# Seven expert steps a layer instead of eight: the four least loaded experts share one step

## The chip, the cores and the metric

The kernel runs on one core of a Trainium2 chip. The metric is the device time of one execution in microseconds (us), the median of several runs. A core has a matrix engine (TensorE, PE in the profile, with its weight loads as PEld), a vector engine (VectorE, DVE), an activation engine (ScalarE, ACT), GpSimd (POOL) and SyncE (SP), which here issues nearly all DMA transfers from memory.

## The reference

Two blocks of a transformer on 256 tokens of width 1024. The first has two layers; each ends in a mixture of experts, and only that part is touched:

```
g_p, g_idx = top_k(softmax(t @ rg_w + rg_b), 1)          # one of 4 groups
e_sel = logits of the 4 experts of that group
top_p, top_i = top_k(softmax(e_sel), 2)                  # 2 of its 4 experts
comb[token, expert] = g_p * top_p / sum(top_p)           # 16 experts, else 0
for each expert e:                                       # width 256
    acc += ((silu(t @ wg[e]) * (t @ wu[e])) @ wd[e]) * comb[:, e]
```

Each token goes to 2 of 16 experts, so 512 token places are spread over 16 experts, unevenly. Worked out from the reference's router on its own inputs, the counts of experts 0 to 15 are 38, 34, 36, 18, 77, 39, 76, 52, 11, 13, 18, 16, 23, 23, 22, 16 in the first layer and 31, 17, 13, 25, 31, 31, 32, 44, 22, 34, 29, 31, 35, 61, 33, 43 in the second. The weights of an expert are 3 MB in fp32.

## The kernel before, in words

The function `moe` does one expert layer. It computes the router, and from it for each token and expert a rank (`rk`, which place of that expert's slots the token gets), a weight (`cw`) and for each expert a count (`cn`). An expert has `CAP` = 64 slots. A *step* handles two experts side by side: expert 0 of the pair in rows 0 to 63 of a PSUM tile, expert 1 in rows 64 to 127, by `tile_position=(0, 64 * e)`, which makes of the 128 columns of TensorE two halves that work side by side. A layer has eight steps:

- `prepare(q)`, once for two steps, makes one-hot slots (`oh`, `ow`) for four experts and gathers their tokens by matmuls (`gps`, line 535, four times 64 slots), into `xg` or `ug`.
- `up(step)` multiplies the gathered tokens by gate and up weights (`gu`, line 557): four weight chunks of 1 MB, two for the first half of the 1024 inputs (one an expert), two for the second half. Within a half the loop runs over four blocks k and, inside, over the experts. Then SiLU on ScalarE and a product on VectorE.
- `turn` transposes the result and the slot weights (`htp`); it stands in the program between the two halves of the next step's `up`.
- `down(step)` multiplies by the down weights (`yp`, line 590, two 1 MB chunks), evicts with the slot weight into a high and a low part (ScalarE line 595, VectorE line 596), and adds the rows back to their tokens by 16 matmuls into four PSUM tiles (`y`, line 599).

The program order is up(0), prepare(1), up(1), down(0), up(2), prepare(2), down(1), up(3), down(2), up(4), prepare(3), down(3) and so on: `down` of a step stands after `up` of the next one. The final order on each engine is set by the framework's planner, which runs the program against modelled costs and takes, of the instructions that it believes ready, the earliest in the program; the order that it finds is fixed in the program.

Weight chunks are read into 13 slots of 1 MB in three pools (`ring` 4, `ring_b` 7, `ring_m` 2); which pool the n-th chunk takes is fixed by the list `rings` (line 989), except those of the last step, which have pools of their own. A chunk's transfer is issued by SP in program order, once the chunk that had its slot before has been used. Steps 0 and 1 take experts 0 to 3. From step 2 on the expert's number is read by SP from `ints`, which VectorE computes: experts 4 to 15 in order, but that the (up to two) experts of most over 64 tokens are exchanged into places 14 and 15, the last step. That step's weights are kept: where any expert has more than 64 tokens, a conditional part (`overflow`, line 774) runs it again for the tokens beyond 64. `more_blocks` computes whether that is so and whether still more blocks are needed. `perm` puts ranks and weights in the same order (`rkp`, `cwp`).

Of the kernel before, what the change touches and what calls it, by code (L numbers as in the profile page):

```python
# [10 lines left out]
F32 = mybir.dt.float32  # L11
# [38 lines left out]
NC1 = _lay(C1T, [("stri", 128), ("cos2d", 128), ("sin2d", 128), ("slot", 64), ("first", 4), ("o14", 16), ("o15", 16), ("free", 16), ("ends", 2), ("less", 16)])  # L50
# [5 lines left out]
FILL = (0, 0, 0, 1, 1, 1, 0, 2, 0)  # L56

# [3 lines left out]
def build(tc, I, O):  # L61
# [3 lines left out]
    with es:  # L65
# [355 lines left out]
        def moe(layer, norm, rc, work, blocks):  # L421
# [85 lines left out]
            def slots(n, ranks, weights):  # L507

                shape = [128, n, CAP]
                oh = small.tile([128, 2, n, CAP], F32R, name="oh", tag=f"oh{n}", bufs=2 if n == 4 else 1)  # L510
                ow = small.tile([128, 2, n, CAP], F32, name="ow", tag=f"ow{n}", bufs=2 if n == 4 else 1)
                for b in range(2):
                    V.tensor_tensor(oh[:, b], C("slot").unsqueeze(1).to_broadcast(shape),
                                    ranks[:, b].unsqueeze(2).to_broadcast(shape), op=ALU.is_equal)
                    V.tensor_tensor(ow[:, b], oh[:, b].bitcast(F32),
                                    weights[:, b].unsqueeze(2).to_broadcast(shape), op=ALU.mult)
                return oh, ow
# [30 lines left out]
            def up(x_, s0, gus, between=lambda: None):  # L548

                gu = acc("gu")  # L550
                for h in range(2):
                    if h:
                        between()
                    w = [gus(h, e) for e in range(2)]
                    for k in range(4):
                        for e in range(2):
                            T.matmul(gu[64 * e:64 * e + 64, :],  # L557
                                     x_[:, 4 * h + k, s0 + 64 * e:s0 + 64 * e + 64],
                                     w[e][:, 512 * k:512 * k + 512],
                                     start=(h == 0 and k == 0), stop=(h == 1 and k == 3),  # L560
                                     tile_position=(0, 64 * e))
# [20 lines left out]
            def down(turned, dns, first, last):  # L582
                ht, back, cws = turned
                wd = [dns(e) for e in range(2)]
                yg = pair([128, D], "yg", small, bufs=2)
                for q in range(2):
                    yp = (ops if q else acc)("yp")
                    for k in range(2):
                        for e in range(2):
                            T.matmul(yp[64 * e:64 * e + 64, :],  # L590
                                     ht[:, 128 * k + 64 * e:128 * k + 64 * e + 64],
                                     wd[e][:, 1024 * k + 512 * q:1024 * k + 512 * q + 512],
                                     start=(k == 0), stop=(k == 1), tile_position=(0, 64 * e))
# [18 lines left out]
            def prepare(q):  # L612
                oh, ow = slots(4, (rkp if q else rk)[:, :, 4 * q:4 * q + 4], (cwp if q else cw)[:, :, 4 * q:4 * q + 4])
                if q == 0:
                    late = t(1, "late")
                    V.scalar_tensor_tensor(late, rk[:, :, 0:1], 0.0, rc.unsqueeze(2), op0=ALU.mult, op1=ALU.add)
                    for q_ in range(2):
                        for b in range(2):
# [10 lines left out]
            order, over, dd = (small.tile([128, 16], F32, name=n, tag=n) for n in ("order", "over", "dd"))  # L629
            top = small.tile([128, 8], F32, name="top", tag="top")  # L630
            two, sw = (small.tile([128, 2], F32, name=n, tag=n) for n in ("two", "sw"))
            V.scalar_tensor_tensor(over, cn, CAP + 0.5, C("free"), op0=ALU.is_gt, op1=ALU.mult)
            V.max(top, over)
            V.scalar_tensor_tensor(two, top[:, 0:2], 0.0, C("ends"), op0=ALU.is_equal, op1=ALU.mult)
            V.tensor_tensor(two, two, top[:, 0:2], op=ALU.add)
            V.scalar_tensor_tensor(dd, iota, two[:, 0:1], C("o15"), op0=ALU.is_equal, op1=ALU.subtract)
            V.tensor_tensor(sw[:, 0:1], iota[:, 15:16], two[:, 0:1], op=ALU.subtract)
            V.scalar_tensor_tensor(order, dd, sw[:, 0:1], iota, op0=ALU.mult, op1=ALU.add)
            V.scalar_tensor_tensor(dd, order, two[:, 1:2], C("o14"), op0=ALU.is_equal, op1=ALU.subtract)
            V.tensor_tensor(sw[:, 1:2], order[:, 14:15], two[:, 1:2], op=ALU.subtract)  # L640
            V.scalar_tensor_tensor(order, dd, sw[:, 1:2], order, op0=ALU.mult, op1=ALU.add)
            ints = small.tile([128, 16], I32, name="ints", tag="ints")
            intr = small.tile([128, 10], I32, name="intr", tag="intr")
            V.tensor_copy(ints, order)

            in2 = small.tile([128, 12, 16], F32, name="in2", tag="in2")
            perm = small.tile([128, 12, 16], F32, name="perm", tag="perm")
            shape = [128, 12, 16]
            V.tensor_tensor(perm, order[:, 4:16].unsqueeze(2).to_broadcast(shape),
                            iota.unsqueeze(1).to_broadcast(shape), op=ALU.is_equal)  # L650
# [8 lines left out]
            def more_blocks():  # L659
# [6 lines left out]
                V.tensor_scalar(ov, cn, CAP + 0.5, None, op0=ALU.is_gt)  # L666
                for n in (2, 3):
                    V.scalar_tensor_tensor(ov, cn, n * CAP + 0.5, ov, op0=ALU.is_gt, op1=ALU.add)
# [27 lines left out]
                V.tensor_tensor(prev, prev, last, op=ALU.subtract)  # L696
                picked(off, prev)
# [36 lines left out]
            def weights_of(step, h, e):  # L734

                if (step, h, e) not in loaded:
                    if step < 2:
                        c = chunk(f"gu{layer}", 4 * step + 2 * e + h) if h < 2 else chunk(f"dn{layer}", 2 * step + e)
                    else:
                        if (step, e) not in experts:  # L740
                            experts[step, e] = value(ints, 2 * step + e)
                        i = experts[step, e]
                        c = dyn(f"gu{layer}", i * 2 + h, ring_b if step == 7 else None) if h < 2 else dyn(f"dn{layer}", i, ring if step == 7 else None)
                    loaded[step, h, e] = c
                return loaded[step, h, e] if step == 7 else loaded.pop((step, h, e))

            hs = {}
            for step in range(9):
                def turned(step=step):
                    if step:  # L750
                        q, h_ = divmod(step - 1, 2)
# [1107 lines left out]
```

## Time and profile before

| | |
|---|---|
| median of 3 runs | 1513.59 us (1512.26 to 1514.64) |
| the profiled execution's own time | 1514.41 us |
| its span, first to last instruction | 1512.7 us |
| TensorE busy | 1474.8 us (97%) |
| VectorE, ScalarE, GpSimd busy | 57%, 44%, 2% |
| moved by DMA | 324.85 MB, mean 215 GB/s |
| granted TensorE clock, mean | 0.986 of full speed |

The page's share of busy time is one over the whole span. The expert layers take from about 183 to 348 us and from about 469 to 619 us of it. Times in the rows are from the span's start. An instruction's shown duration on TensorE holds its way through the pipeline, so that neighbours overlap: what it costs is the distance to the next one's start. In a row of a stretch the busy times stand in the order PE, PEld, DVE, ACT, POOL, each with its number of instructions in brackets; in a row of a timeline the start comes first, then how long the run of x instructions lasted.

### The profile page before, as it was taken

What the parts mean: (1) busy time and instruction counts of PE and PEld (TensorE: products, weight loads), DVE (VectorE), ACT (ScalarE), POOL (GpSimd) and SP (SyncE); (2) the same over time, 40 slices, a digit from 0 to 9 for tenths busy, and PEclk for the clock granted to TensorE, in tenths of its full rate; (3) what the DMA queues carried; (4) which work ended last, traced back from release to release, by engine and by line L of the source; (5) the groups of instructions that cost most, each with busy time, mean ns of one, the idle gap of its engine ahead of it and who ended that gap; (6) DMA issues with size and microseconds to landing.
All of it is one profiled execution on the core that took longest, in us unless ns stands there. A gap on an engine that the chain in (4) does not pass through costs nothing.

```text
span 1512.7 us, 25576 instructions
## 1 busy us (share of the span) xinstructions
PE 1474.8 (97%) x10412; PEld 1178.0 (78%) x10412; DVE 857.9 (57%) x1682; ACT 658.1 (44%) x1114; POOL 26.7 (2%) x59
## 2 busy tenths in 40 slices
PE   8999899989999999899999999999999999999998
PEld 3756645445986444698789999999898789999998
DVE  2765452225646222657777775555758777765554
ACT  2544311115433111556564554444565654654443
POOL 0000000000000000010000000000010000000000
PEclk9999999999999999999999999999999999999999
DMA  9974789739584986553315464554444135465540
GB/s 396 388 296 167 304 368 404 292 136 371 205 349 174 414 336 246 178 171 116 136 59 186 177 221 175 188 196 167 136 157 168 57 114 184 177 223 179 185 166 29
DMA packets 47005, 324.85 MB, mean 215 GB/s; under 512 B 5600, under 2 KB 5984, under 8 KB 8480
## 3 DMA queue, kind: packets, MB, share of 16 engines
q1 hardware_dynamic: 45360, 320.12, 55.8%
q8 instruction: 86, 1.41, 0.4%
q10 hardware_dynamic: 1296, 1.55, 0.3%
q0 software_dynamic: 224, 1.46, 0.3%
q14 instruction: 39, 0.32, 0.1%
HBM read 322.06 MB, written 1.05 MB: 214 GB/s over the span
## 4 chain that ended last, share of the span: by engine, by line
PE 56%; DVE 2%; ACT 1%; issue 0%; DVEq 0%; ACTq 0%
PE fm L162 10%; PE fm L163 10%; PE fm L161 10%; PE d L162 4%; PE d L161 4%; PE d L163 4%; PE tm L194 1%; PE tm L195 1%; PE tm L196 1%; PE sp L1486 1%; PE lf L162 1%; PE lf L163 1%; PE lf L161 1%; PE po L1475 1%; PE ptp L1469 1%; DVE sc L1359 1%
## 5 line engine op out<-in xcount | busy, mean ns | idle before, releaser
L134 DVE TENSOR_TENSOR wlo<-w,whi 128x1024 fp32r<-128x1024 f32 (+1 forms) x314 | 378.4, 1208 | 251.9 <-ACT whi L133 249.2
L133 ACT CAST whi<-w 128x1024 fp32r<-128x1024 f32 (+1 forms) x314 | 324.3, 1035 | 384.5 <-PE fm L162 230.7
L161 PE MATMUL fm<-acth,whi 128*128 128x256 f32 x592 | 169.4, 286 | 0.0
L162 PE MATMUL fm<-actl,whi 128*128 128x256 f32 x592 | 168.3, 284 | 0.0
L163 PE MATMUL fm<-acth,wlo 128*128 128x256 f32 x592 | 167.9, 284 | 0.0
L163 PE MATMUL d<-hidh,wlo 128*128 128x256 f32 x512 | 144.2, 282 | 0.0
L162 PE MATMUL d<-hidl,whi 128*128 128x256 f32 x512 | 144.0, 281 | 0.0
L161 PE MATMUL d<-hidh,whi 128*128 128x256 f32 x512 | 143.9, 281 | 0.0
L162 PE MATMUL fm<-oTl,whi 128*128 128x256 f32 x512 | 143.6, 281 | 0.0
L163 PE MATMUL fm<-oTh,wlo 128*128 128x256 f32 x512 | 143.3, 280 | 0.0
L161 PE MATMUL fm<-oTh,whi 128*128 128x256 f32 x512 | 143.1, 280 | 0.0
L162 PEld LDWEIGHTS fm<-actl,whi 128*128 128x128 f32 x592 | 112.5, 190 | 2.3 <-issue 2.3
L161 PEld LDWEIGHTS fm<-acth,whi 128*128 128x128 f32 x592 | 113.2, 191 | 1.0 <-issue 0.8
L163 PEld LDWEIGHTS fm<-acth,wlo 128*128 128x128 f32 x592 | 112.4, 190 | 1.3 <-issue 1.0
L162 PEld LDWEIGHTS fm<-oTl,whi 128*128 128x128 f32 x512 | 96.8, 189 | 0.4 <-DVE oTl L1100 0.4
L162 PEld LDWEIGHTS d<-hidl,whi 128*128 128x128 f32 x512 | 96.7, 189 | 0.4 <-DVE hidl L134 0.4
L161 PEld LDWEIGHTS fm<-oTh,whi 128*128 128x128 f32 x512 | 96.9, 190 | 0.0
L161 PEld LDWEIGHTS d<-hidh,whi 128*128 128x128 f32 x512 | 96.8, 189 | 0.1
L163 PEld LDWEIGHTS d<-hidh,wlo 128*128 128x128 f32 x512 | 96.7, 189 | 0.1
L163 PEld LDWEIGHTS fm<-oTh,wlo 128*128 128x128 f32 x512 | 96.7, 189 | 0.0
L590 PE MATMUL yp<-w,ht 128*64 128x512 f32 x272 | 84.1, 646 | 6.8 <-PEq L774 3.5
L557 PE MATMUL gu<-w,xg 128*64 128x512 f32 x288 | 70.1, 599 | 0.0
(537 smaller groups left out, 2904.5 us busy)
## 6 DMA issues: line engine op xcount, KB each, us to landing
w<-gu SPq DMA_DIRECT2D x64, 1024.0 KB, 9.3
w<-mod SPq DMA_DIRECT2D x48, 1024.0 KB, 11.2
w<-dn SPq DMA_DIRECT2D x32, 1024.0 KB, 9.7
w<-gw SPq DMA_DIRECT2D x32, 1024.0 KB, 4.8
w<-up SPq DMA_DIRECT2D x32, 1024.0 KB, 4.8
w<-dw SPq DMA_DIRECT2D x32, 1024.0 KB, 4.8
w<-tm SPq DMA_DIRECT2D x12, 1024.0 KB, 5.0
w<-oin SPq DMA_DIRECT2D x8, 1024.0 KB, 8.3
```

The lines of the kernel that those rows point to most:

```text
L133: A.copy(hi, src)
L134: V.tensor_sub(lo, src, hi.bitcast(F32))
L161: T.matmul(out, ws[0], xs[0], start=first, stop=False, skip_group_check=skip)
L162: T.matmul(out, ws[0], xs[1], start=False, stop=False, skip_group_check=skip)
L163: T.matmul(out, ws[1], xs[0], start=False, stop=last, skip_group_check=skip)
L194: T.matmul(ps, at[0], ww[0], start=first, stop=False, skip_group_check=True)
L195: T.matmul(ps, at[1], ww[0], start=False, stop=False, skip_group_check=True)
L196: T.matmul(ps, at[0], ww[1], start=False, stop=k == NK - 1, skip_group_check=True)
L557: T.matmul(gu[64 * e:64 * e + 64, :], x_[:, 4 * h + k, s0 + 64 * e:s0 + 64 * e + 64], w[e][:, 512 * k:512 * k + 512], start=(h == 0 and k ...
L590: T.matmul(yp[64 * e:64 * e + 64, :], ht[:, 128 * k + 64 * e:128 * k + 64 * e + 64], wd[e][:, 1024 * k + 512 * q:1024 * k + 512 * q + 512] ...
L1359: V.scalar_tensor_tensor(dst, rl[:, :nk], iw[:, b, h:h + 1], dst, op0=ALU.mult, op1=ALU.add)
L1469: T.transpose(tp[:, 128 * c:128 * c + 128], prs[g][:, 128 * c:128 * c + 128], ident)
```

## The change

Two sizes of step. The order of experts 4 to 15 is now a full sort on VectorE: `more_` counts for each how many of the twelve have more tokens (`key` breaks ties by number), and `RANKS` says which rank comes to which place. The four with the fewest (ranks 8 to 11) come to places 8 to 11 and form one step (step 4) with 32 slots each; the two with the most still come to the last step, which is now step 6. `up` and `down` take a number of experts n: with n = 4 each expert's tile is 32 columns wide, `tile_position=(0, 32 * e)`, and such a step reads 8 gate/up chunks and 4 down chunks. The gather is made for 64 slots an expert as before, and the step uses the first 32 of them. An expert of the four with more than 32 tokens goes to the conditional part. The prepare of the last quarter stands after up(4) as before, and its tokens are now used in step 5 and not 6.

```diff
-NC1 = _lay(C1T, [("stri", 128), ("cos2d", 128), ("sin2d", 128), ("slot", 64), ("first", 4), ("o14", 16), ("o15", 16), ("free", 16), ("ends", 2), ("less", 16)])
+NC1 = _lay(C1T, [("stri", 128), ("cos2d", 128), ("sin2d", 128), ("slot", 64), ("first", 4), ("rank", 12), ("gap", 38), ("less", 16)])
...
+STEPS = ((0, 1), (2, 3), (4, 5), (6, 7), (8, 9, 10, 11), (12, 13), (14, 15))
+PART = ((0, 0), (0, 1), (1, 0), (1, 1), (2, 0), (3, 0), (3, 1))
+LAST = 6
+RANKS = (2, 3, 4, 5, 8, 9, 10, 11, 6, 7, 1, 0)
...
-            def slots(n, ranks, weights):
+            def slots(n, ranks, weights, cap=CAP):
...
-                ow = small.tile([128, 2, n, CAP], F32, name="ow", tag=f"ow{n}", bufs=2 if n == 4 else 1)
+                ow = small.tile([128, 2 * n * CAP], F32, name="ow", tag=f"ow{n}", bufs=2 if n == 4 else 1)
+                ow = ow[:, 0:2 * n * cap].rearrange("p (b n s) -> p b n s", b=2, n=n)
...
-                    V.tensor_tensor(ow[:, b], oh[:, b].bitcast(F32),
-                                    weights[:, b].unsqueeze(2).to_broadcast(shape), op=ALU.mult)
+                    V.tensor_tensor(ow[:, b], oh[:, b, :, 0:cap].bitcast(F32),
+                                    weights[:, b].unsqueeze(2).to_broadcast([128, n, cap]), op=ALU.mult)
...
-            def up(x_, s0, gus, between=lambda: None):
...
+            def up(x_, s0, gus, between=lambda: None, n=2):
...
+                each = 128 // n
...
-                    w = [gus(h, e) for e in range(2)]
+                    w = [gus(h, e) for e in range(n)]
...
-                        for e in range(2):
-                            T.matmul(gu[64 * e:64 * e + 64, :],
-                                     x_[:, 4 * h + k, s0 + 64 * e:s0 + 64 * e + 64],
+                        for e in range(n):
+                            T.matmul(gu[each * e:each * e + each, :],
+                                     x_[:, 4 * h + k, s0 + CAP * e:s0 + CAP * e + each],
...
-                                     tile_position=(0, 64 * e))
+                                     tile_position=(0, each * e))
...
-            def down(turned, dns, first, last):
+            def down(turned, dns, first, last, n=2):
...
-                wd = [dns(e) for e in range(2)]
+                each = 128 // n
+                wd = [dns(e) for e in range(n)]
...
-                        for e in range(2):
-                            T.matmul(yp[64 * e:64 * e + 64, :],
-                                     ht[:, 128 * k + 64 * e:128 * k + 64 * e + 64],
+                        for e in range(n):
+                            T.matmul(yp[each * e:each * e + each, :],
+                                     ht[:, 128 * k + each * e:128 * k + each * e + each],
...
-                                     start=(k == 0), stop=(k == 1), tile_position=(0, 64 * e))
+                                     start=(k == 0), stop=(k == 1), tile_position=(0, each * e))
...
-                oh, ow = slots(4, (rkp if q else rk)[:, :, 4 * q:4 * q + 4], (cwp if q else cw)[:, :, 4 * q:4 * q + 4])
+                oh, ow = slots(4, (rkp if q else rk)[:, :, 4 * q:4 * q + 4], (cwp if q else cw)[:, :, 4 * q:4 * q + 4],
+                               CAP // 2 if q == 2 else CAP)
...
-            order, over, dd = (small.tile([128, 16], F32, name=n, tag=n) for n in ("order", "over", "dd"))
-            top = small.tile([128, 8], F32, name="top", tag="top")
-            two, sw = (small.tile([128, 2], F32, name=n, tag=n) for n in ("two", "sw"))
-            V.scalar_tensor_tensor(over, cn, CAP + 0.5, C("free"), op0=ALU.is_gt, op1=ALU.mult)
-            V.max(top, over)
-            V.scalar_tensor_tensor(two, top[:, 0:2], 0.0, C("ends"), op0=ALU.is_equal, op1=ALU.mult)
-            V.tensor_tensor(two, two, top[:, 0:2], op=ALU.add)
-            V.scalar_tensor_tensor(dd, iota, two[:, 0:1], C("o15"), op0=ALU.is_equal, op1=ALU.subtract)
-            V.tensor_tensor(sw[:, 0:1], iota[:, 15:16], two[:, 0:1], op=ALU.subtract)
-            V.scalar_tensor_tensor(order, dd, sw[:, 0:1], iota, op0=ALU.mult, op1=ALU.add)
-            V.scalar_tensor_tensor(dd, order, two[:, 1:2], C("o14"), op0=ALU.is_equal, op1=ALU.subtract)
-            V.tensor_tensor(sw[:, 1:2], order[:, 14:15], two[:, 1:2], op=ALU.subtract)
-            V.scalar_tensor_tensor(order, dd, sw[:, 1:2], order, op0=ALU.mult, op1=ALU.add)
+            order, key, more_ = (small.tile([128, 16], F32, name=n, tag=n) for n in ("order", "key", "more"))
+            few = small.tile([128, 24], F32, name="few", tag="few")[:, 0:16]
+            V.scalar_tensor_tensor(key, cn, 16.0, iota, op0=ALU.mult, op1=ALU.add)
+            in2 = small.tile([128, 12, 16], F32, name="in2", tag="in2")
+            perm = small.tile([128, 12, 16], F32, name="perm", tag="perm")
+            G.memset(perm, 0.0)
+            G.memset(more_, 0.0)
+            shape = [128, 12, 12]
+            V.tensor_tensor(in2[:, :, 0:12], key[:, 4:16].unsqueeze(1).to_broadcast(shape),
+                            key[:, 4:16].unsqueeze(2).to_broadcast(shape), op=ALU.is_gt)
+            V.tensor_reduce(more_[:, 4:16], in2[:, :, 0:12], axis=AX.X, op=ALU.add)
+            V.tensor_tensor(perm[:, :, 4:16], more_[:, 4:16].unsqueeze(1).to_broadcast(shape),
+                            C("rank").unsqueeze(2).to_broadcast(shape), op=ALU.is_equal)
+            shape = [128, 12, 16]
+            V.tensor_tensor(in2, perm, iota.unsqueeze(1).to_broadcast(shape), op=ALU.mult)
+            V.tensor_reduce(order[:, 4:16], in2, axis=AX.X, op=ALU.add)
...
-            V.tensor_copy(ints, order)
...
-            in2 = small.tile([128, 12, 16], F32, name="in2", tag="in2")
-            perm = small.tile([128, 12, 16], F32, name="perm", tag="perm")
-            shape = [128, 12, 16]
-            V.tensor_tensor(perm, order[:, 4:16].unsqueeze(2).to_broadcast(shape),
-                            iota.unsqueeze(1).to_broadcast(shape), op=ALU.is_equal)
+            V.tensor_copy(ints[:, 4:16], order[:, 4:16])
...
-                V.tensor_scalar(ov, cn, CAP + 0.5, None, op0=ALU.is_gt)
...
+                V.tensor_scalar(few, more_, 7.5, None, op0=ALU.is_gt)
+                V.scalar_tensor_tensor(key, few, CAP / 2, cn, op0=ALU.mult, op1=ALU.add)
+                V.tensor_scalar(ov, key, CAP + 0.5, None, op0=ALU.is_gt)
...
-                    V.scalar_tensor_tensor(ov, cn, n * CAP + 0.5, ov, op0=ALU.is_gt, op1=ALU.add)
+                    V.scalar_tensor_tensor(ov, key, n * CAP + 0.5, ov, op0=ALU.is_gt, op1=ALU.add)
...
+                V.scalar_tensor_tensor(prev, few, 0.5, prev, op0=ALU.mult, op1=ALU.add)
...
-                            experts[step, e] = value(ints, 2 * step + e)
+                            experts[step, e] = value(ints, STEPS[step][e])
...
-                        c = dyn(f"gu{layer}", i * 2 + h, ring_b if step == 7 else None) if h < 2 else dyn(f"dn{layer}", i, ring if step == 7 else None)
+                        c = (dyn(f"gu{layer}", i * 2 + h, ring_b if step == LAST else None) if h < 2 else
+                             dyn(f"dn{layer}", i, ring if step == LAST else None))
...
-                return loaded[step, h, e] if step == 7 else loaded.pop((step, h, e))
+                return loaded[step, h, e] if step == LAST else loaded.pop((step, h, e))
...
-            for step in range(9):
+            for step in range(LAST + 2):
...
-                        q, h_ = divmod(step - 1, 2)
+                        q, h_ = PART[step - 1]
+                        n = len(STEPS[step - 1])
...
-                                            lambda b: ow[:, b, 2 * h_:2 * h_ + 2].rearrange("p e s -> p (e s)"))
+                                            lambda b: ow[:, b, n * h_:n * h_ + n].rearrange("p e s -> p (e s)"))
...
-                if step < 8:
-                    q, h_ = divmod(step, 2)
-                    hs[step] = up(quarter[q][0], 128 * h_, lambda h, e: weights_of(step, h, e), turned)
+                if step <= LAST:
+                    q, h_ = PART[step]
+                    hs[step] = up(quarter[q][0], 128 * h_, lambda h, e: weights_of(step, h, e), turned,
+                                  len(STEPS[step]))
...
-                        weights_of(7, 2, e)
+                        weights_of(LAST, 2, e)
...
-                        overflow(res, cwp[:, :, 14:16], lambda h, e: weights_of(7, h, e), lambda e: weights_of(7, 2, e))
+                        overflow(res, cwp[:, :, 14:16], lambda h, e: weights_of(LAST, h, e),
+                                 lambda e: weights_of(LAST, 2, e))
...
-                    yg = down(hs.pop(step - 1), lambda e: weights_of(step - 1, 2, e), step == 1, step == 8)
-            for key in [k for k in loaded if k[0] == 7]:
+                    yg = down(hs.pop(step - 1), lambda e: weights_of(step - 1, 2, e), step == 1, step == LAST + 1,
+                              len(STEPS[step - 1]))
+            for key in [k for k in loaded if k[0] == LAST]:
...
+    put(c1, C1T, "rank", np.array(RANKS)[None])
```

## Rows read from the trace of the kernel before

**Rows 1.** Page: busy us of each engine, share of the span, instructions

```profile
PE 1474.8 (97%) x10412; PEld 1178.0 (78%) x10412; DVE 857.9 (57%) x1682; ACT 658.1 (44%) x1114; POOL 26.7 (2%) x59
```

**Rows 2.** Stretches of both expert layers: busy us (instructions), clock, DMA share, GB/s

```profile
189.90:317.70 127.80, 127.06 (x624) 58.31 (x624) 42.67 (x129) 21.04 (x38) 0.00 (x0) 1.00 0.85 339
476.60:604.50 127.90, 127.15 (x625) 58.48 (x624) 42.45 (x129) 21.03 (x38) 0.00 (x0) 1.00 0.83 329
...
200.00:270.00 70.00, 69.85 (x362) 33.92 (x362) 23.21 (x63) 12.74 (x24) 0.00 (x0) 1.00 0.99 404
```

**Rows 3.** TensorE's timeline, one late step in each layer: start us, us

```profile
287.06 7.09 PE L557 MATMUL gu<-w,ug 128*64 128x512 f32 x32
293.98 1.88 PE L590 MATMUL yp<-w,ht 128*64 128x512 f32 x4
...
296.37 3.65 PE L590 MATMUL yp<-w,ht 128*64 128x512 f32 x12
...
302.17 0.28 PE L599 MATMUL y<-back,ygh 128*128 128x256 f32 x1
302.29 0.28 PE L599 MATMUL y<-back,ygl 128*128 128x256 f32 x1
302.50 7.09 PE L557 MATMUL gu<-w,ug 128*64 128x512 f32 x32
...
573.69 7.09 PE L557 MATMUL gu<-w,ug 128*64 128x512 f32 x32
...
589.13 7.09 PE L557 MATMUL gu<-w,ug 128*64 128x512 f32 x32
```

**Rows 4.** TensorE's timeline: matmuls of 32 columns, a down in two-wide order

```profile
464.59 2.78 PE L375 MATMUL mps<-w,cpad 128*32 128x512 f32 x22
...
531.80 3.60 PE L590 MATMUL yp<-w,ht 128*64 128x512 f32 x16
```

**Rows 5.** TensorE's timeline, step 4 of the first layer, its gather, step 5

```profile
256.15 3.65 PE L557 MATMUL gu<-w,xg 128*64 128x512 f32 x16
259.74 0.74 PE L535 MATMUL gps<-oh,whi 128*128 128x256 f32 x4
...
271.75 2.79 PE L557 MATMUL gu<-w,xg 128*64 128x512 f32 x10
...
278.55 1.88 PE L590 MATMUL yp<-w,ht 128*64 128x512 f32 x4
```

**Rows 6.** SP's timeline: issues of weight chunks, and time to landing (line 717)

```profile
192.83 2.71 SPq L717 DMA_DIRECT2D w<-gu  x4
...
227.01 8.51 SPq L717 DMA_DIRECT2D w<-dn  x2
...
236.36 9.34 SPq L717 DMA_DIRECT2D w<-gu  x4
...
DMA to landing us min/median/max: 4.7/9.1/14.1
```

**Rows 7.** VectorE's timeline: the order of the experts; TensorE's next gather

```profile
187.86 0.17 DVE L633 MAX8 top<-over 128x8 f32<-128x16 f32 x1
...
191.38 0.17 DVE L644 CAST ints<-order 128x16 int32<-128x16 f32 x1
...
194.35 0.42 DVE L513 TENSOR_TENSOR oh<-cst,rkp 128x256 fp32r<-128x256 f32 x1
...
198.25 0.74 PE L535 MATMUL gps<-oh,whi 128*128 128x256 f32 x4
```

**Rows 8.** TensorE's timeline: around the conditional part, first and second layer

```profile
318.06 1.08 PE L535 MATMUL gps<-oh,whi 128*128 128x128 f32 x8
...
340.71 4.54 PE L590 MATMUL yp<-w,ht 128*64 128x512 f32 x10 [3.49 <-PEq L774]
...
604.37 0.28 PE L599 MATMUL y<-back,ygl 128*128 128x256 f32 x1
607.45 1.97 PE L590 MATMUL yp<-w,ht 128*64 128x512 f32 x4 [2.80 <-PEq L772]
```

More of the change, by code (lines that the diff above doesn't have):

```diff
@@ L1826, in host_layout @@
     put(c, CT, "inv", np.tile(np.concatenate([fr(16), fr(32), fr(8)]), 2)[None])
-    put(c1, C1T, "o14", (r(16) == 14)[None])
-    put(c1, C1T, "o15", (r(16) == 15)[None])
-    put(c1, C1T, "free", np.where(r(16) >= 4, r(16), 0)[None])
+    put(c1, C1T, "rank", np.array(RANKS)[None])
     put(c1, C1T, "less", np.tri(4, k=-1).reshape(1, 16))
-    put(c1, C1T, "ends", np.array([15, 14])[None])
     put(c1, C1T, "first", np.array([4.0, 3.0, 2.0, 1.0])[None])
```

## The prediction

> **What bounds the kernel now.** The page comes first: TensorE is busy 97% of the span [rows 1], so it looks as if TensorE's own instructions are the time. That is an average, so next come the stretches of the two expert layers, the only stage that the change touches. From 189.9 to 317.7 us TensorE works 127.06 of 127.80 us, the granted clock is 1.00 of full (its 2.4 GHz level), and the second layer repeats it to 0.1 us [rows 2]. VectorE and ScalarE work a third and a sixth of that. DMA is the second resource: over the first 70 us of it its engines are busy 99% at 404 GB/s, over the whole stretch 85% [rows 2]. TensorE is hardly ever kept waiting for a chunk all the same, as its 0.74 us of idle time leave no room for it: the 13 slots keep the weights ahead. So in this stage a TensorE instruction that goes is time that goes, as long as the weights still come in time.
>
> The timeline of TensorE then gives the price of a step. Late steps, without a gather, repeat at equal distance: from the `gu` at 287.06 to that at 302.50 in the first layer, from 573.69 to 589.13 in the second, 15.44 us both times [rows 3].
>
> **What a tile width costs.** The runs show how matmuls share the array. A run of 32 `gu` records takes 7.09 us, 16 `yp` records in two-wide order 3.60, so 16 more records take 3.49 us [rows 3, 4]; but only 4 `yp` records also take 1.88 us, which is half of 16 and not a quarter [rows 3]. These agree if two neighbours on the two halves of the array share one slot of time: (7.09 - 3.60) / 8 = 0.436 us a slot, 0.11 over, and 4 unpaired records make 4 slots, 1.85. The 12 that follow in 3.65 us fill 8 slots: 4 pairs and 4 alone. The kernel also has matmuls of 32 columns, those of the conditions, on four quarters: 22 records in 2.78 us [rows 4], that is (2.78 - 0.11) / 0.436 = 6.1 slots, four to a slot. So 64 records of a four-wide `up` fill 16 slots, as 32 records of a two-wide one do, and it costs the same 6.92 us; 32 `yp` records fill 8 slots.
>
> **The change part by part.**
>
> *One step less.* Eight steps become seven a layer. Steps 0 to 3 keep their place, step 4 is wider at equal cost, the old steps 6 and 7 follow it. What goes is one late step: 16 slots of `gu`, 12 of `yp`, one `htp`, 16 `y` matmuls and the small gaps between, 15.44 us [rows 3]. Two layers: 30.9 us. This is all on the path, as TensorE is what everything waits for [rows 2].
>
> *Order of the four-wide matmuls.* They share slots only where four experts' records stand side by side in the fixed order. In the program they do. The planner breaks that where it believes one chunk late: the late downs show it, with one expert's 4 records alone, then `htp` (which stands later in the program), then the rest, 12 slots for 8 [rows 3]. The ups of the same steps, 32 records in 7.09 us, are whole, and so is the earlier down at 531.80 [rows 4]. Step 4 asks for 8 chunks where it asked for 4, just before the place where the first split down stands (278.55, rows 5). Bounds: no split at all, and `yp` of step 4 back from 12 to 8 slots: 1.7 us less a layer than above. Or every expert by itself: `gu` in runs of 8 records of one quarter, where only the last of a run shares a slot with the first of the next, 64 - 7 = 57 slots for 16, and `yp` in runs of 4, 32 - 7 = 25 for 12: 54 slots, 23.5 us more a layer. I take the nearest row, one split of the kind at 293.98 to 296.37 in `gu` (4 slots) and the 12 slots of today in `yp`: 1.7 us a layer, 3.5 in all.
>
> The Trainium skill, in "TensorEngine Tiling (Array Packing)", section "Tiling Modes", says that changing the tile configuration, and not only the tile, drains TensorE. The step adds changes between 32 and 64 columns where neighbours were 64 wide. If each cost a whole slot, by this rule, three new ones a layer would bring the sum to about 1489. The rows have such a change too, from 128 to 64 columns: from one `y` matmul to the next it takes 0.12 us, from the last `y` to the `gu` 0.21 [rows 3], so 0.09 us a change, and by that the sum stays.
>
> *Weights in time.* The bytes are the same, 48 MB a layer, in 15.4 us less. From 192.83 us on, 38 chunks are left, the first four those of step 2 [rows 6]. At 404 GB/s [rows 2] a chunk (1.049 MB) takes 2.6 us: 99 us, so the last could land at about 292 plus its latency of 9 [rows 6], 301; the last `down` of the first layer would begin at 340.71 - 15.4 = 325 [rows 8]. In the second layer the same stream begins 286.6 us later (573.69 - 287.06), ends at about 587, and the last down begins at 607.45 - 15.4 = 592. So the stream as such does not bound, with 5 us to spare. The tightest place inside is step 4. The pool of the n-th chunk does not change, so it goes out when the n-th did before: the wide step's chunks 5 to 8 take the places of two `dn` (from 227.01) and two `gu` (from 236.36, four over 9.34 us, so by 241) [rows 6]. With the median landing that is 250, with the longest of 14.1 us 255, and the second half of `up` begins at 256.15 [rows 5]: in time. Two `dn` and the four `gu` of step 5 follow, six times 2.6 us later, by 266, and its main run begins at 271.75 [rows 5]. I take nothing for it; the price, if cover is short, is 2.6 us a chunk, at most the four chunks that step 4 asks for early: 10 us a layer.
>
> *Gather of the last quarter.* It still runs after `up` of step 4 (259.74, rows 5). Its user moves from step 6 to step 5, whose main run starts 12 us later. Nothing.
>
> *Sorting.* Between `MAX8` and the cast to `ints` VectorE ran nine small operations on 16 elements or fewer in 3.5 us, part of it evictions in between [rows 7]. New are six up to the cast: one on 16 elements, three on 144 and two on 192 elements, at 0.17 to 0.4 us each (a cast on 16 takes 0.17, an `oh` on 256 takes 0.42) [rows 7], some 1.8 us; `perm` leaves the part behind the cast. That is a change of -1 to +1 us. Behind it wait SP's first chunk of step 2 (192.83) and the one-hots of the next gather, ready at 194.35 + 0.42 while TensorE comes to that gather at 198.25: 3.5 us of cover [rows 7]. Two memsets go to an idle GpSimd (2%, rows 1). `ow` gets smaller by half for one quarter, `more_blocks` gets two operations more, both off the path. Nothing.
>
> *Sum.* The profiled execution took 1514.41 us, 1.7 over its span and 0.8 over the median of 1513.59. 1514.41 - 30.9 + 3.5 = 1487.0; against the median 1486.2. I predict 1486.
>
> **The rivals.**
>
> *The planner takes the wide step apart.* One mechanism, in the order of TensorE in step 4: its eight `gu` chunks are believed to come one by one, and the matmuls are emitted expert by expert, on one quarter at a time. For it: the split downs at and after the very place where more weights are asked for. Against it: every `up` is whole, even in steps whose down is split [rows 3], and a chunk that is believed late shows as one split, not as a run of them. It decides from 15.44 / 0.436 = 35 extra slots a layer; fully apart, it costs 23.5 us a layer and the kernel is slower: 1513.6 + 2 x (23.5 - 15.4) = 1530. Half of it, about 11 us, leaves 1505.
>
> *The stream of weights becomes the bound.* For it: DMA at 99% over 70 us [rows 2] and the same bytes in less time. Against it: the sums above. If step 4 and its successors wait for 10 us a layer, 1483 + 20 = 1503.
>
> *It does not do what it says.* 32 slots are too few, and the conditional part runs in the second layer too. There it cost 340.71 - 318.06 = 22.7 us in the first layer, of which 3 are the branch that the second layer pays as well (607.45 - 604.37) [rows 8]: 19.6 us, so 1506. Against it: the four fewest of experts 4 to 15 have 16, 16, 13, 11 tokens in the first layer and 31, 31, 29, 22 in the second; it fits by one.
>
> **How the numbers follow.** The three runs spread by 0.16%, so less than 0.2% (3 us) can't be told from no change. The forecast, seven whole or nearly whole steps at 1477 to 1495, gets 0.70. Planner apart: 0.19, of which 0.11 partly, 1495 to 1511, and 0.08 from there to 1530. Stream bound: 0.07, between the forecast and 1503. Overflow: 0.02. What I have not thought of: 0.02, slower. From 1478 to 1502 leaves out 0.05 below and about 0.14 above. Faster: 0.70 + 0.07 + 0.02 and 0.09 of the planner's partial case, 0.88; same: 0.02 of that case and 0.02 of the worse one, 0.04; slower: 0.06 + 0.02 = 0.08.
>
> **What would show it.** TensorE's timeline should have, in each layer, 64 `gu` and 32 `yp` records of 32 columns, the `gu` in 6.9 to 9 us of its time; the last down begins 14 to 17 us earlier in the first layer and twice that in the second, and all behind it moves with it. Starts in fours within a few hundredths of a us prove a slot shared by four; lone 32-column records 0.43 us apart prove the split. A wait of `gu` or `yp` for the DMA of `w` shows the stream as the bound. A second run of the conditional part shows as a gather of 128 columns at the end of the second layer. The prediction is wrong if either layer gets shorter by less than 12 us.

## The result: 20 us less where 28 were forecast

The changed kernel takes 1493.7 us (1490.45 to 1495.34, 4 runs) against 1514.12 us of the kernel before (1512.26 to 1515.65, 4 runs) on the same chip: a ratio of 0.9866, 95% interval 0.9852 to 0.9879, that is 18.3 to 22.4 us less. The forecast was 1486, with a range of 1478 to 1502. The sign and the mechanism came as forecast, but two terms of the sum were too small: broken groups of matmuls cost 8.7 us where 3.5 were reckoned, and the gathers some 2 us where nothing was. Below, a difference between two kernels is that of their ratios to the kernel before, where 0.001 is 1.5 us. The profiled execution took 1494.22 us, its span was 1492.5. A matmul of the program shows as two records in these traces: an `up` of two experts is 16 matmuls and 32 records.

The page of the changed kernel: busy us of each engine, share of the span, instructions. It answers to [rows 1]: TensorE has 21.7 us less to do and is still busy 97%.

```profile
PE 1453.1 (97%) x10370; PEld 1168.0 (78%) x10372; DVE 851.7 (57%) x1666; ACT 654.1 (44%) x1108; POOL 27.3 (2%) x63
```

A stretch of the changed kernel, columns as in [rows 2], whose row of before had the same busy time of TensorE, and a DMA share of 0.99 with 404 GB/s:

```profile
200.00:270.00 70.00, 69.85 (x378) 32.96 (x378) 22.00 (x64) 11.28 (x22) 0.00 (x0) 1.00 0.96 391
```

TensorE is as busy here as before, 69.85 of 70 us at the full clock. What it did not save must be in its own instructions, and its timeline shows where. This is step 4 of the first layer (start us, us, then the run of instructions), from its `up` to its `down`:

```profile
251.68 1.04 PE L566 MATMUL gu<-w,xg 128*32 128x512 f32 x2
...
253.57 1.05 PE L566 MATMUL gu<-w,xg 128*32 128x512 f32 x4
...
257.00 3.62 PE L566 MATMUL gu<-w,xg 128*32 128x512 f32 x26
...
261.23 1.04 PE L566 MATMUL gu<-w,xg 128*32 128x512 f32 x2
...
263.81 3.63 PE L566 MATMUL gu<-w,xg 128*32 128x512 f32 x30
267.37 1.93 PE L600 MATMUL yp<-w,ht 128*64 128x512 f32 x4
269.24 0.44 PE L580 MATMUL htp<-cst,hh 128*128 128x128 f32 x2
...
269.82 3.65 PE L600 MATMUL yp<-w,ht 128*64 128x512 f32 x12
...
275.93 7.09 PE L566 MATMUL gu<-w,ug 128*64 128x512 f32 x32
282.95 1.90 PE L600 MATMUL yp<-w,ht 128*32 128x512 f32 x4
...
285.37 3.66 PE L600 MATMUL yp<-w,ht 128*32 128x512 f32 x28
```

The `up` of step 4 has its 64 records of 32 columns, but in five pieces. With the prediction's slot (0.436 us, and 0.11 over for a run) the pieces are 2, 2, 8, 2 and 8 slots: 22, where whole groups take 16. A short run is dear: 2 records take as long as 8 could. The `down` of step 3 (267.37 and 269.82) is in two pieces with `htp` (269.24) between, 12 slots for 8, and the `up` of step 5 behind it (275.93) is whole. The `down` of step 4 is in two pieces too, 12 slots, as forecast. The second layer repeats all of this.

The same steps were not whole before either. TensorE's timeline of the kernel before: the first half of step 4's `up` (its second half is at 256.15 in [rows 5]), then step 3's `down` and the `up` of step 5:

```profile
250.07 1.07 PE L557 MATMUL gu<-w,xg 128*64 128x512 f32 x2
...
251.99 3.65 PE L557 MATMUL gu<-w,xg 128*64 128x512 f32 x14
...
262.74 1.07 PE L590 MATMUL yp<-w,ht 128*64 128x512 f32 x2
...
264.88 1.50 PE L590 MATMUL yp<-w,ht 128*64 128x512 f32 x5
...
266.64 1.89 PE L590 MATMUL yp<-w,ht 128*64 128x512 f32 x8
...
269.83 1.08 PE L557 MATMUL gu<-w,xg 128*64 128x512 f32 x4
...
275.06 3.65 PE L557 MATMUL gu<-w,xg 128*64 128x512 f32 x16
```

Step 4's `up` took 2 + 8 + 8 = 18 slots. Step 3's `down` took 2 slots at 262.74 and, with a `yp` and two early `gu` of step 5 between its runs of 5 and 8, 8 more to 268.5; the rest of step 5's `up` took 2, 6 (271.75 in [rows 5]) and 8: 26 for both, where whole groups take 24. So the change added 4 slots in the `up` of step 4 (22 for 18), and 2 in the `down` of step 3 and the `up` of step 5 (28 for 26).

At the start of a layer there is more of it. The ups of steps 0 and 1 in the changed kernel, first layer:

```profile
189.53 1.93 PE L566 MATMUL gu<-w,xg 128*64 128x512 f32 x6
...
192.53 6.22 PE L566 MATMUL gu<-w,xg 128*64 128x512 f32 x26
...
202.10 1.07 PE L566 MATMUL gu<-w,xg 128*64 128x512 f32 x2
...
204.23 3.65 PE L566 MATMUL gu<-w,xg 128*64 128x512 f32 x14
```

Six records in 1.93 us are 4 slots and 26 in 6.22 are 14, 18 for 16; 2 and 14 records in 1.07 and 3.65 us are 2 and 8, again 2 over. Before, both ups filled 16. Counted in this way from the first `gu` to the last `down` ahead of the conditional part, a layer had 205 slots before and has 187 now. A late step is 28 slots [rows 3], so 177 were to be left: 4 + 2 + 4 = 10 slots a layer are lost, where the forecast took 4. `gu` and `yp` together take 83.9 us a layer after 91.7, from start to start: 18 slots less, and not 28.

The ends of the two layers, rows that answer to [rows 8]: the gather of the conditional part, and the first matmul behind the second layer's branch. They come 10.86 and 18.13 us earlier; 15.44 us less 10 slots is 11.1 a layer. The second layer by itself, from its first `gu` (476.61 before, 467.77 now), got 9.3 us shorter.

```profile
307.20 1.08 PE L543 MATMUL gps<-oh,whi 128*128 128x128 f32 x8
...
589.32 5.01 PE L600 MATMUL yp<-w,ht 128*64 128x512 f32 x16 [2.87 <-PEq L788]
```

### The profile page after: what moved, and what is told of

It is laid out like the page before. It is cut to its first block, busy times and chain, and to the rows that moved or that the text cites. A ratio compares the mean times of both kernels' runs of the same rounds, so it can differ in the third digit from the quotient of the medians.

```text
span 1492.5 us, 25477 instructions
## 1 busy us (share of the span) xinstructions
PE 1453.1 (97%) x10370; PEld 1168.0 (78%) x10372; DVE 851.7 (57%) x1666; ACT 654.1 (44%) x1108; POOL 27.3 (2%) x63
## 4 chain that ended last, share of the span: by engine, by line
PE 57%; DVE 2%; ACT 1%; issue 0%; DVEq 0%; ACTq 0%
PE fm L169 10%; PE fm L170 10%; PE fm L168 10%; PE d L169 4%; PE d L168 4%; PE d L170 4%; PE sp L1504 1%; PE tm L201 1%; PE tm L202 1%; PE tm L203 1%; PE lf L169 1%; PE lf L170 1%; PE lf L168 1%; PE po L1493 1%; PE ptp L1487 1%; DVE wlo L141 1%
## 5 line engine op out<-in xcount | busy, mean ns | idle before, releaser
L600 PE MATMUL yp<-w,ht 128*64 128x512 f32 (+1 forms) x272 | 71.8, 622 | 6.6 <-PEq L791 3.2
L566 PE MATMUL gu<-w,ug 128*64 128x512 f32 x256 | 62.2, 598 | 0.0
```

The lines of the kernel that those rows point to most:

```text
L566: T.matmul(gu[each * e:each * e + each, :], x_[:, 4 * h + k, s0 + CAP * e:s0 + CAP * e + each], w[e][:, 512 * k:512 * k + 512], start=(h = ...
L600: T.matmul(yp[each * e:each * e + each, :], ht[:, 128 * k + each * e:128 * k + each * e + each], wd[e][:, 1024 * k + 512 * q:1024 * k + 51 ...
```

## The experiments

Four theories for the missing 8 us. **A**: broken groups; matmuls on different columns share a slot only as neighbours, and the fixed order separates them. **B**: the weight stream holds TensorE up. **C**: a group of four needs longer than a slot. **D**: the sort's own operations delay something.

What TensorE waited for in the first layer of the changed kernel (engine, line, waited for: us in all, times, longest) already speaks against B. In its rows there is no chunk of weights (the two left out are gathers that wait for VectorE ahead of the first `gu`, as before the change), and of the waits of the `gu` instructions by themselves (second fence: us, times) 0.2 us are for DMA, no more than before.

```profile
...
PE y L609 <- DVE ygl L606: 0.7, 3, 0.3
PE gps L543 <- ACT ug L549: 0.2, 1, 0.2
```

```profile
  DMA w<-dn: 0.2, 1
```

**1. Step 4's `up` with its last expert first.** The eight chunks of step 4 are issued one after the other over 24 us (row below, SP of the changed kernel). The program lists the experts in the order of these issues, so by A the first expert's matmuls are ready alone. Here the last comes first.

```profile
217.83 24.47 SPq L730 DMA_DIRECT2D w<-gu  x8
```

```diff
-                        for e in range(n):
+                        for e in (range(n) if n == 2 else (3, 0, 1, 2)):
```

> In step 4 alone the inner loop of `up` takes the expert whose chunk comes last first (3, 0, 1, 2). Theory A (slots): the missing gain is groups of matmuls that the planner broke in TensorE's fixed order, while the chunks have in truth landed. The order now has step 4's 64 records in whole groups of four, 182 slots a layer for 190: 8 x 0.436 x 2 = 7 us less than the changed kernel's 1493.7, so about 1487, and no new wait for `w`. Theory B (stream): the chunks of step 4 do come late; TensorE then waits for the last chunk ahead of the group, and the time stays at 1492 to 1495. Theory C (width): four-wide slots cost more than two-wide ones, and the order changes nothing: 1492 to 1495, with starts in fours more than 0.43 us apart.

Measured: 1487.74 us (1484.23 to 1488.36), ratio 0.9833 (0.9816 to 0.9851), 5.0 us less than the changed kernel. TensorE's timeline of this kernel:

```profile
255.98 0.74 PE L543 MATMUL gps<-oh,whi 128*128 128x256 f32 x4 [1.08 <-ACT ug L549]
...
257.11 3.64 PE L566 MATMUL gu<-w,xg 128*32 128x512 f32 x32
...
264.11 3.64 PE L566 MATMUL gu<-w,xg 128*32 128x512 f32 x32
267.68 3.65 PE L600 MATMUL yp<-w,ht 128*64 128x512 f32 x16
...
272.64 1.07 PE L566 MATMUL gu<-w,ug 128*64 128x512 f32 x2
```

The `up` is whole: 32 records of 32 columns in 3.64 us are 8 slots of four, which refutes C. The `down` of step 3 became whole with it. Two things are given back: step 5's `up` now breaks (272.64, 2 slots), and the gather, no longer interspersed with `gu`, waits twice 1.08 us (the first is shown) for ScalarE to empty its PSUM tile. In all 8 slots a layer less, 7.0 us, and 3.3 us more of that wait over both layers: 3.7, against 5.0 measured.

**2. The downs with the last expert first.**

```diff
-                        for e in range(n):        # in down
+                        for e in reversed(range(n)):
```

> In every `down` the inner loop takes the last expert first. Theory A: the late downs become whole, 178 slots a layer for 190 (from the trace of the changed kernel, where step 4's down took 12 slots and not 16, 8 to 12 less): 7 to 10.5 us less than 1493.7, so 1483 to 1487. Theory B: `yp` waits for the last `dn` chunk, 1491 to 1495. Theory C says nothing of two-wide downs: at most 2 us from step 4's.

Measured: 1489.62 us (1486.33 to 1491.63), ratio 0.985 (0.9831 to 0.9869), 2.4 us less than the changed kernel, below what was expected. The downs of steps 3, 4 and 5 are whole, 12 slots a layer less, and that of step 0 takes 1 less. But the ups of steps 5 and 6 now break (274.53), 2 slots each: 9 slots a layer less remain, 7.8 us in all. And TensorE stands still where it did not:

```profile
268.99 0.44 PE L580 MATMUL htp<-cst,hh 128*128 128x128 f32 x2 [1.04 <-DVE hh L574]
...
269.58 3.65 PE L600 MATMUL yp<-w,ht 128*64 128x512 f32 x16
...
274.53 1.07 PE L566 MATMUL gu<-w,ug 128*64 128x512 f32 x2
```

`htp` transposes `hh`, the product that VectorE makes of `gu` after ScalarE's SiLU, and directly behind `gu` it must wait 1.04 us for it. In the kernel before, four lone `yp` records stood in that gap [rows 3]: the split cost 4 slots, 1.74 us, and covered 1 us. The wait appears three times more in each layer, 4.0 us against 1.0 in the first and 3.3 against none in the second. 7.8 less 6.3 is 1.5, against 2.4 measured. The intervals of the two ratios reach 2.9 and 2.0 us to either side, so the times alone do not tell the gain from none; what was traded for what is read from the traces.

**3 and 4. All ups and downs with the last expert first,** in the changed kernel and, as 4, in the kernel before. The pair tells what a step is worth when the groups are whole in both.

```diff
-                        for e in range(n):        # in up and in down; 4: range(2), then (1, 0)
+                        for e in reversed(range(n)):
```

> In every `up` and `down` the inner loop takes the last expert first. Theory A: all groups are whole, 160 slots a layer for 186 to 190: 26 to 30 slots, 23 to 26 us less than 1493.7, so 1468 to 1471, unless the stream of weights becomes the bound on the way, which would show as idle time of TensorE until a DMA of `w`. Theory B: TensorE waits for chunks instead, 1488 to 1495. Theory C: the two-wide steps gain, step 4 does not: about 1475.

> The kernel before, eight steps, with the last expert first in every `up` and `down`. Theory A: 184 slots a layer for 206: 22 x 0.436 x 2 = 19 us less than 1514, so 1495; then the pure worth of one step less is the distance to the run with seven steps and the same order, 24 slots and 3 us of `y` a layer, about 27 us. Theory B and C: the kernel before has no wide step and a stream that keeps ahead; by B (late chunks are real) it stays at 1510 to 1515.

Measured: 3 took 1474.62 us (1471.54 to 1477.76), ratio 0.9748 (0.9729 to 0.9767); 4 took 1501.49 us (1497.69 to 1505.01), ratio 0.9925 (0.9908 to 0.9941). Both gain less than expected, for the reason found in 2: what TensorE waited for in the first layer of 3, and then of 4 (one wait for `hh` in each is in the conditional part, and was there before):

```profile
PE htp L580 <- DVE hh L574: 3.0, 3, 1.0
PE gps L543 <- ACT ug L549: 2.3, 3, 1.1
```

```profile
PE htp L571 <- DVE hh L565: 4.0, 4, 1.0
```

Between them lie 26.8 us. A late step of 15.44 us [rows 3] without its 4 broken slots is 13.7, twice that 27.4. So the first term of the prediction, a step less, was of the right size; the change just did not get the whole of it while its groups were broken. In the fixed order of 3 a layer has 160 slots, 27 less than in the changed kernel: 23.5 us. The waits for `hh` and for the gather's tile are 7.4 us longer over both layers and those for `ygl` 0.9 shorter, which leaves 17.0; measured are 17.9. For 4 it is 184 slots, 21 less than before, 18.3 us, less 6.0 of waits for `hh`: 12.3, against 11.4 measured.

**5. The sort alone.** Eight steps of two, as before, with the full sort of experts.

```diff
+STEPS = ((0, 1), (2, 3), (4, 5), (6, 7), (8, 9), (10, 11), (12, 13), (14, 15))
...
-            V.tensor_copy(ints, order)
+            V.tensor_reduce(order[:, 4:16], in2, axis=AX.X, op=ALU.add)
...
+            V.tensor_copy(ints[:, 4:16], order[:, 4:16])
```

> Eight two-wide steps as before, with only the full sort of experts 4 to 15 added. Theory A (order): the sort moves the conversion to integers in the planner's timing, so that ups 0 and 1 come apart into one more group each, 4 to 6 slots of 0.436 us a layer: 3.5 to 5 us slower than the kernel before, about 1516 to 1517 against 1512 to 1514, and the two pieces of up 0 and up 1 are seen in TensorE's timeline. Rival D (the sort's own operations on VectorE hold something up): slower by as much, but with a wait of TensorE for VectorE or of SP for the integers in the rows and ups 0 and 1 whole. Rival N (the sort costs nothing, what it seemed to cost comes with the wide step): within 1 us of before.

**6. The wide step without the sort.** The exchange of before in the changed kernel; of an expert in places 8 to 11 the tokens beyond 32 are left out.

```diff
-            V.tensor_reduce(order[:, 4:16], in2, axis=AX.X, op=ALU.add)
...
+            V.scalar_tensor_tensor(order, dd, sw[:, 1:2], order, op0=ALU.mult, op1=ALU.add)
...
-            V.tensor_copy(ints[:, 4:16], order[:, 4:16])
...
+            V.tensor_copy(ints, order)
```

> The changed kernel with the exchange of before in place of the full sort: experts stay in their numbers' order, so that places 8 to 11 hold whatever expert comes there and its tokens beyond 32 are left out. The instructions of the steps are the same. Theory A: ups 0 and 1 are whole again, 4 slots a layer less: 3.5 us faster than the changed kernel, about 1490; up 4 and the split downs stay. Rival N: no difference from the changed kernel. Rival D: 3 us or so faster, with ups 0 and 1 in the same pieces as in the changed kernel.

Measured: 5 took 1517.36 us (1514.96 to 1521.52), ratio 1.0032 (1.0017 to 1.0047), 4.8 us slower than before. 6 took 1486.94 us (1484.79 to 1488.32), ratio 0.9832 (0.9816 to 0.9848), 5.1 us faster than the changed kernel. TensorE's timeline of 5 (second layer) and of 6 (first layer):

```profile
479.44 1.93 PE L566 MATMUL gu<-w,xg 128*64 128x512 f32 x6
...
482.43 6.22 PE L566 MATMUL gu<-w,xg 128*64 128x512 f32 x26
...
492.00 1.07 PE L566 MATMUL gu<-w,xg 128*64 128x512 f32 x2
```

```profile
188.87 1.08 PE L566 MATMUL gu<-w,xg 128*64 128x512 f32 x4
...
191.02 6.23 PE L566 MATMUL gu<-w,xg 128*64 128x512 f32 x28
...
201.53 3.65 PE L566 MATMUL gu<-w,xg 128*64 128x512 f32 x16
```

With the sort, 6 + 26 and 2 + 14 records; without it, 4 + 28 and 16. That is the 4 slots a layer, 3.5 us in all, and it lies within the intervals of both differences. Some of the rest is in the traces too: the second layer of 5 has 2 slots more in the `down` of step 3 and the `up` of step 5, and in 6 the gathers no longer wait for `ug`, 1.2 us in the changed kernel. D falls: VectorE has the integers no later than before. The sort's cast in its timeline, in the changed kernel; the cast began at 191.38 in [rows 7]:

```profile
190.91 0.17 DVE L658 CAST ints<-order 128x12 int32<-128x12 f32 x1
```

**7. Step 4's `up` expert by expert,** the rival of the prediction made by hand.

```diff
-                    for k in range(4):
-                        for e in range(n):
+                    for k, e in ([(k, e) for e in range(n) for k in range(4)] if n == 4 else
+                                 [(k, e) for k in range(4) for e in range(n)]):
```

> The changed kernel, but in step 4's up the loop over experts stands outside that over the four blocks, so that the records of one expert stand side by side: aaaabbbbccccdddd and so on. Theory A (a slot of 0.436 us is shared only by neighbours on different quarters): some 34 slots more a layer, 68 in all, 29.6 us: 1523, slower than the kernel before by 9 us, with 64 records of 32 columns 0.43 us apart but for one at each change of expert. Rival C (the quarters overlap whatever the order, and the changed kernel's loss lies elsewhere): within 3 us of the changed kernel. Rival B (the weight stream bounds the wide step): less than half of the 30 us, since the wait for weights would have covered part of it.

Measured: 1512.82 us (1510.09 to 1514.21), ratio 1.0001 (0.999 to 1.0012): 20.4 us slower than the changed kernel, and the whole gain of the change is gone. TensorE's timeline:

```profile
251.12 1.05 PE L567 MATMUL gu<-w,xg 128*32 128x512 f32 x2
...
253.02 6.26 PE L567 MATMUL gu<-w,xg 128*32 128x512 f32 x22
...
259.57 3.62 PE L567 MATMUL gu<-w,xg 128*32 128x512 f32 x8
...
265.36 5.37 PE L567 MATMUL gu<-w,xg 128*32 128x512 f32 x16
...
272.73 5.37 PE L567 MATMUL gu<-w,xg 128*32 128x512 f32 x16
279.09 0.44 PE L581 MATMUL htp<-cst,hh 128*128 128x128 f32 x2 [0.99 <-DVE hh L575]
```

The runs are 2, 14, 8, 12 and 12 slots, 48 against 22. The `down` of step 3 is whole again (4 slots less) and pays 0.99 us for `hh`: 22 slots and 1 us a layer, 21.2 us in all, as the second layer repeats it, and 20.4 measured. A is confirmed, and its price of a slot, but the number of slots expected was too large: 16 records of two experts one behind the other take 12 slots and not 15. Half of the run of 8 shares its time with the next expert's.

**8. Everything last first, and `htp` behind half a `down`.** Kernel 3, with the first transpose of `turn` bound to come after the last `yp` of the running down's first half, so that these lie over the wait for `hh`.

```diff
+                    ins = T.transpose(tp[:, 128 * q:128 * q + 128], hh[:, 128 * q:128 * q + 128], ident)
+                    if q == 0 and behind[0] is not None:
+                        tc.add_manual_dep(ins.ins, behind[0].ins.name, ...)    # order only
...
+                    if q == 0 and pin:
+                        behind[0] = last_yp
...
+                              len(STEPS[step - 1]), 0 < step < LAST)
```

> All loops over experts from the last to the first, as in the run at 1474.6, and the first transpose of turn bound to come behind the first half of the running down, so that 1.88 us or more of that down lie over the wait for SiLU and product. Theory A with the wait as the second term: up to 1.0 us for each of two or three steps a layer, 4 to 6 us less than that run: 1469 to 1472. Rival: the binding only moves the transposes, and the down of the next step waits for what stood behind them: 1474 to 1478.

Measured: 1472.06 us (1471.01 to 1472.88), ratio 0.9735 (0.972 to 0.9749), 2.0 us less than kernel 3 and the lowest of all. The intervals of the two overlap and reach 2.2 and 2.9 us to either side, so the times alone do not tell 2.0 us from none. 4 to 6 us were expected. TensorE's timeline and its waits in the first layer:

```profile
277.20 3.64 PE L606 MATMUL yp<-w,ht 128*32 128x512 f32 x32
...
292.04 0.44 PE L582 MATMUL htp<-cst,hh 128*128 128x128 f32 x2 [1.00 <-DVE hh L574]
```

```profile
PE htp L582 <- DVE hh L574: 2.0, 2, 1.0
```

One wait of 1.0 us a layer is gone (2.0 left of 3.0 in the first layer), which for two layers is as much as the difference measured. It is that of step 5, whose `htp` now stands behind the `yp` at 277.20. The other in the steps (292.04) is that of the last step, 6. The edit does not reach it: `pin` is set for `0 < step < LAST` alone, so that the `down` ahead of the last step's transposes binds nothing, and `htp` stands right behind `gu` as in kernel 3. The wait in the conditional part and the gather's 2.3 us stayed as well. Whether binding the last step's transposes gives its 1.0 us too was not tried.

## Why the prediction was right, and where a size was off

*One step less, 15.44 us a layer:* right. Seven steps, with 32-column records that fill a slot by fours where they stand together; experiments 3 and 4 give 26.8 us where 27.4 follow from whole steps.

*Order of the four-wide matmuls, taken as 4 slots a layer:* too small by 2 slots a layer, 1.7 us in all. The `up` of step 4 got the 4 slots that were forecast for it (22 for 18), and its `down` the 12; the 2 in the `down` of step 3 and the `up` of step 5 were not seen. That the 4 came out is in part luck, as the row it leaned on did not hold: "every `up` is whole" is true of the late steps of [rows 3], but the `up` of step 4, the one to be replaced, stood in pieces of 2, 14 and 16 records, and the split `down` at 278.55 was not the first, as step 3's was in pieces ahead of it. Against whole groups, the measure that the prediction meant, step 4's `up` lost 6. The rival "the planner takes the wide step apart" was thus half right, the mechanism without its extent; and it was priced too high: in experiment 7 the `up` expert by expert takes 48 slots for 16, 32 over, where the rival reckoned 57, 41 over.

*Weights in time, nothing:* right; 0.2 us of waiting in the first layer, as before, with 5 us reckoned as spare.

*Sorting, nothing:* the mis-sized term. Right on VectorE and wrong on TensorE: 4 slots a layer in the ups of steps 0 and 1, 3.5 us, and in the time of the whole kernel 4.8 and 5.1 us by experiments 5 and 6. It was looked at for what waits for it, not for what it does to the planner's order two engines away. That the order moves with the sort is shown; by which modelled cost the planner came to it is not.

*Gather of the last quarter, nothing:* wrong by a little. In the second layer 0.9 us more of waiting for ScalarE's `ug` appears, and over both layers all gathers take 28.2 us from start to start instead of 27.4, as they stand in more pieces.

*The sum:* with 10 slots a layer it is 1514.4 - 30.9 + 8.7 = 1492.2, and the profiled execution took 1494.22. Of the 2.0 us left, the gathers' time and their waits for `ug` are 1.8.

*A change of tile width, 0.09 us:* right. In experiment 1 the 32 `gu` of 32 columns begin at 264.11 and the 64-column `yp` at 267.68, 3.57 us for 8 slots of 0.436, so 0.08 over. The Trainium skill, "TensorEngine Tiling (Array Packing)", "Tiling Modes", has such a change drain the engine; the trace shows no more than these 0.08 us.

*What was to show it:* the 64 and 32 records of 32 columns came, four to a slot in whole runs and one or two to a slot in the short ones. The condition "wrong if either layer gets shorter by less than 12 us" was met: the first layer's mark came 10.9 us earlier, and the second layer got 9.3 us shorter. Its last down began 18.1 us earlier, where twice 14 to 17 us was said. By its own yardstick the prediction of the two layers failed, although the time lies in the range.

## What to carry to other kernels

In every run here, matmuls that share the array by columns did so only as neighbours in the fixed order, so count runs and not instructions: a piece of two records costs as much as eight in fours. Count the kernel before in the same way, as a step that looks whole in one place may be broken in another, and look at what a new computation does to the fixed order of other engines, not only at who waits for it. List the operand that arrives last first in such a loop, then all of its group are ready together (experiment 3: 187 slots a layer become 160). And before a broken group is mended, ask what its lone matmuls cover: in experiment 2, 6.3 of the 7.8 us saved came back as a wait for the vector product behind them.

## What had not been expected of the hardware

Matmuls of two experts one behind the other on different quarters of the array overlap in part: 16 records in 5.37 us, 12 slots (experiment 7).

The falls of the granted clock move with the kernel. Between the expert layers, in the attention part with the same instructions in both, this is the changed kernel and then the one before (columns as in [rows 2]):

```profile
415.00:425.00 10.00, 9.29 (x70) 6.46 (x63) 0.54 (x3) 0.59 (x1) 0.00 (x0) 0.82 1.01 424
425.00:435.00 10.00, 10.00 (x75) 10.00 (x75) 3.66 (x5) 4.49 (x6) 0.00 (x0) 0.84 1.01 426
```

```profile
425.00:435.00 10.00, 9.29 (x84) 5.75 (x77) 1.08 (x4) 0.59 (x1) 0.00 (x0) 1.00 0.95 361
```

Both had 0.7 us of idle TensorE there (9.29 busy of 10), ahead of the same `m` matmul, at 419.46 and 430.42. Only the changed kernel's clock fell behind it: a mean of 0.83 over 20 us, which mixes the levels of 1.2 and 2.4 GHz and costs 3.4 us. That is part of why the second layer's mark moved by only 7.3 us more than the first one's: the second layer began 8.8 us earlier, after the first one's end had come 10.9 us earlier. Summed over the pieces of 5 us of the span in which the clock was under 0.97, its lost share is 21.5 us in the kernel before and 21.7 in the changed one, so the difference of their times is not made by it.
